# First mixer of a two-block model: projections laid between the delta rule's steps, inverses built from 64x64 blocks, output projection in two halves

## The chip, the core and the metric

The kernel runs on one core of one Trainium2 chip. The metric is the device time of one execution in microseconds (us). TensorE is written PE in the rows (its weight loads PEld), VectorE DVE, ScalarE ACT, GpSimd POOL, and SyncE, which issues most DMAs, SP.

## What is computed

The reference chains two blocks of two layers over 256 tokens (272 with 16 learned ones in front) of width 1024. In the first block a layer is a feed-forward, a mixer and a second feed-forward. The change touches the mixer of layer 0 alone:

```python
def hybrid_attention_mixer(h, w_in, fox_bf, conv_w, a_log, dt_bias, o_gain, w_out):
    fq, fk, fv, ff, gqkv, ga, gb, gz = split_cols(h @ w_in, HYB_SIZES)
    o_fox = forgetting_attention(q_f, k_f, v_f, log_f)[:, :, PAD:]      # 8 heads of 64
    gqkv = jax.nn.silu(causal_depthwise_conv(gqkv, conv_w))
    ...
    o_gdn = gated_delta_rule(q_g, k_g, v_g, log_g, beta)[:, :, PAD:].transpose(0, 2, 1, 3)   # 4 heads of 128
    o_gdn = rms_norm(o_gdn, o_gain) * jax.nn.silu(gz...)
    o = jnp.concatenate([o_fox, o_gdn.reshape(B_, L, GDN_VW)], axis=-1)
    return o @ w_out

def gated_delta_rule(q, k, v, log_g, beta):          # chunks of 128 tokens
    lower = jnp.where(strict, jnp.einsum('bhnid,bhnjd->bhnij', kb, k) * decay, 0.0)
    sol = lax.linalg.triangular_solve(lower, rhs, left_side=True, lower=True, unit_diagonal=True)
    ...
    def step(S, inp):                                # one chunk after the other
        u = u_b - jnp.einsum('bhck,bhkv->bhcv', w_c, S)
        o = jnp.einsum('bhck,bhkv->bhcv', qd, S) + jnp.einsum('bhij,bhjv->bhiv', a_c, u)
        S = S * dl[..., None, None] + jnp.einsum('bhck,bhcv->bhkv', kd, u)
```

## The kernel before, in words

Activations lie feature-major: eight tiles `h[m]` of 128 features by 272 tokens. A matrix product in full precision is three matmuls (`mm3`, lines 105 to 107), since each operand is split into a high and a low part. `wload` (lines 68 to 82) brings a block of weights of 128 x 1024 by DMA into one of four buffers `w`; ACT copies it, 512 columns at a time, to `wh` (line 78), and DVE subtracts that for `wl` (line 79); there are four halves of each. A projection of 128 outputs is thus one DMA, two casts, two subtractions and 24 matmuls of 272 columns into an accumulator of the pool "mm", which has three; all smaller products go to the pool "sm", which has four.

The method `_hybrid` writes the mixer in Python program order, and the tile framework then orders each engine's queue and places the waits; the engines take their queues strictly in order. First come 28 projections: `conv(j)` for twelve blocks of the delta rule's queries, keys and values, `fox(j)` for twelve of the attention's (0 to 3 queries, 4 to 7 keys, 8 to 11 values), and four of `gate`. Short follow-up work is queued by `after(n, f)` and run by the n+1st next `tick`, one tick for each projection: squares and norms (`squared`, `square`, `factors`, `frows`), scaling of queries and keys by four broadcast products for each delta head (`scaled`, line 568), the products inside a chunk (`products`, line 583) and transposes (`turned`). What is still due at the end runs in the loop `while self.due`.

The 272 tokens are the chunks 0, 1 and 2 of 16, 128 and 128. `chunk(i)` inverts a chunk's unit triangular matrices for the four delta heads with `inverse`: from blocks of 1 it doubles up to 128 in seven levels; each level takes a product with `LT` (line 838), a copy of the result to `ivx` on ACT, a second product (line 844), a masked copy on DVE and a transpose (`flip`, lines 827 and 828). `recur` then goes through the chunks: state times keys (672), the inverse applied (678), the state's update (688, 694), the output (698, 699). `finish(i)` norms a chunk's output: squares, sums (714), an inverse root on DVE (lines 160 to 165), diagonals (721), a broadcast product (724), and the scaling and splitting (726 to 729). `attend(j, i)` does one pair of attention heads for one chunk of queries: logits of both heads into two "mm" accumulators (742 to 745), the maximum (746), the exponential (752), transposes (763, 768) and the product with the values (776).

All of these are generators that yield between steps, and the loops at the end of `_hybrid` call them in turn: while there are inverses, the three chunks in each round and one of two attention tasks (pairs 0 and 1, pairs 2 and 3) in every other round; afterwards the recurrence, its norms and the attention. Only then comes the output projection: eight blocks of 24 matmuls (`hyb_w_out`), each added to `h[m]`. `doubled` (line 863) is a second way to invert, for 64x64 blocks, two on the diagonal of a tile, which the RWKV mixer of layer 1 uses; its products (line 873) are pairs of 64x64 matmuls.

## Time and profile before

| | |
|---|---|
| three runs | 3681.22, 3685.11, 3688.15 us; median 3685.11 |
| the profiled execution | 3671.75 us, its span 3669.9 us |
| TensorE matmuls | busy 3590.3 us (98%), 31745 |
| TensorE weight loads | busy 3409.7 us (93%) |
| DVE | busy 2773.0 us (76%) |
| ACT | busy 1942.3 us (53%) |
| POOL | busy 289.1 us (8%) |
| DMA | 561.54 MB, mean 153 GB/s |
| mean granted clock of TensorE | 0.983 of full speed |

The span runs from the first to the last instruction. Matmuls are pipelined and their ends are modelled, so neighbouring ones overlap, and the distance between two starts, not the duration of one, is what a matmul costs in a stream. A busy TensorE can run at either of its two clock levels (2.4 and 1.2 GHz); the granted clock is their mean over a stretch, as a share of the higher.

### The profile page before, as it was taken

The page shows a single profiled execution, that of the slowest core. Times are in us where ns is not written, and L with a number is a line of the kernel's source. Part 1 is how long each engine was busy: PE and PEld are TensorE (multiplying, and loading weights), DVE is VectorE, ACT ScalarE, POOL GpSimd, SP SyncE. Part 2 cuts the span into 40 slices and gives each one's busy share as a digit, 9 for nine tenths or more (in the row PEclk, how much of TensorE's full clock was granted, in tenths as well). Part 3 has the DMA queues.
Part 4 walks back from the last instruction along what each step waited for, and adds up shares of the span by engine and source line. Part 5 has one row for each costly group of instructions (what it writes and reads, how often), then busy time and mean ns, then how long its engine had stood idle before and what let it go on. Part 6 is the DMA issues. An engine that isn't in the chain of part 4 may idle for free. (4 is left out here: it accounts for less than half of the span.)

```text
span 3669.9 us, 80619 instructions
## 1 busy us (share of the span) xinstructions
PE 3590.3 (98%) x31745; PEld 3409.7 (93%) x31745; DVE 2773.0 (76%) x6198; ACT 1942.3 (53%) x4100; POOL 289.1 (8%) x374
## 2 busy tenths in 40 slices
PE   8999999999998999999999999999999999999998
PEld 8999799998898999999999999999989999998887
DVE  6666576667856877788987788657788998788866
ACT  5554355555632557655554444556765555444454
POOL 2111021110201101011000000001011000000000
PEclk9999799999998999999999999999999999999999
DMA  5552055554310565445554444555435555555554
GB/s 184 173 167 81 24 171 172 175 173 127 108 37 25 181 187 172 138 144 168 176 183 164 162 162 161 173 184 164 151 124 182 174 173 173 163 166 173 168 187 150
DMA packets 158426, 561.54 MB, mean 153 GB/s; under 512 B 18715, under 2 KB 21163, under 8 KB 158045
## 3 DMA queue, kind: packets, MB, share of 16 engines
q1 hardware_dynamic: 157628, 555.07, 46.6%
q8 instruction: 248, 4.06, 0.5%
q0 software_dynamic: 416, 1.32, 0.1%
q14 instruction: 134, 1.09, 0.1%
HBM read 555.27 MB, written 1.05 MB: 152 GB/s over the span
## 5 line engine op out<-in xcount | busy, mean ns | idle before, releaser
L78 ACT CAST wh<-w 128x512 fp32r<-128x512 f32 (+1 forms) x2102 | 1292.3, 617 | 1244.3 <-PE mm L106 732.1
L79 DVE TENSOR_TENSOR wl<-w,wh 128x512 fp32r<-128x512 f32 (+1 forms) x2102 | 1461.2, 698 | 559.6 <-ACT wh L78 527.4
L105 PE MATMUL mm<-xh,wh 128*128 128x256 f32 (+2 forms) x4032 | 1162.0, 288 | 12.4 <-ACT wh L78 11.6
L107 PE MATMUL mm<-xh,wl 128*128 128x256 f32 (+2 forms) x4032 | 1152.3, 286 | 21.5 <-DVE wl L79 21.4
L106 PE MATMUL mm<-xl,wh 128*128 128x256 f32 (+2 forms) x4032 | 1141.6, 283 | 0.1
L107 PEld LDWEIGHTS mm<-xh,wl 128*128 128x128 f32 x4032 | 764.2, 190 | 26.9 <-DVE wl L79 25.9
L105 PEld LDWEIGHTS mm<-xh,wh 128*128 128x128 f32 x4032 | 766.5, 190 | 14.9 <-ACT wh L78 12.6
L106 PEld LDWEIGHTS mm<-xl,wh 128*128 128x128 f32 x4032 | 767.8, 190 | 1.8 <-issue 0.6
L2209 PE MATMUL mm<-ah,wh 128*128 128x256 f32 x768 | 219.3, 286 | 0.0
L2209 PE MATMUL mm<-al,wh 128*128 128x256 f32 x768 | 216.9, 283 | 0.0
L2209 PE MATMUL mm<-ah,wl 128*128 128x256 f32 x768 | 215.7, 281 | 0.0
L105 PE MATMUL sm<-xh,wh 128*128 128x272 f32 (+4 forms) x744 | 214.4, 288 | 0.2 <-ACT aa L1072 0.2
L107 PE MATMUL sm<-xh,wl 128*128 128x272 f32 (+4 forms) x744 | 214.1, 288 | 0.0
L106 PE MATMUL sm<-xl,wh 128*128 128x272 f32 (+4 forms) x744 | 213.5, 287 | 0.0
L105 PE MATMUL mm<-ah,wh 128*128 128x272 f32 (+1 forms) x704 | 201.5, 286 | 0.0
L107 PE MATMUL mm<-ah,wl 128*128 128x272 f32 (+1 forms) x704 | 201.4, 286 | 0.0
L106 PE MATMUL mm<-al,wh 128*128 128x272 f32 (+1 forms) x704 | 201.3, 286 | 0.0
L2211 PE MATMUL mm<-wh,ah 128*128 128x512 f32 x384 | 153.5, 400 | 0.0
L2211 PE MATMUL mm<-wh,al 128*128 128x512 f32 x384 | 152.1, 396 | 0.0
L2211 PE MATMUL mm<-wl,ah 128*128 128x512 f32 x384 | 151.1, 394 | 0.0
L2209 PEld LDWEIGHTS mm<-ah,wl 128*128 128x128 f32 x768 | 145.0, 189 | 0.0
L2209 PEld LDWEIGHTS mm<-al,wh 128*128 128x128 f32 x768 | 144.7, 188 | 0.2 <-DVE al L2200 0.2
(866 smaller groups left out, 6774.9 us busy)
## 6 DMA issues: line engine op xcount, KB each, us to landing
w<-p_u SPq DMA_DIRECT2D x256, 512.0 KB, 3.5
w<-p_v SPq DMA_DIRECT2D x256, 512.0 KB, 3.5
w<-ffn_in SPq DMA_DIRECT2D x176, 512.0 KB, 3.5
w<-m_w_in SPq DMA_DIRECT2D x96, 512.0 KB, 3.5
w<-ffn_out SPq DMA_DIRECT2D x64, 448.0 KB, 3.3
w<-ffn_out SPq DMA_DIRECT2D x32, 512.0 KB, 3.5
w<-p_wq SPq DMA_DIRECT2D x32, 512.0 KB, 3.7
w<-hyb_w SPq DMA_DIRECT2D x28, 512.0 KB, 3.5
```

What stands on the lines that cost most here:

```text
L78: self.at_s = nc.scalar.copy(wh, w[:rows, s:e])
L79: self.at_v = nc.vector.tensor_tensor(wl, w[:rows, s:e], wh, op=OP.subtract)
L105: mm(out, wh, xh, start=start, stop=False)
L106: mm(out, wh, xl, start=False, stop=False)
L107: self.at_t = mm(out, wl, xh, start=False, stop=stop)
L2209: M(po[m // 2][:, m % 2 * T : m % 2 * T + T], w_[:, m * P : (m + 1) * P], a_, **flags)
L2211: M(po[m // 2], a_[:, i * P : (i + 1) * P], w_[:, f * 512 : f * 512 + 512], **flags)
```

## The change

Five things are done, all in `_hybrid` and the helpers it calls.

1. Six of the twelve attention projections (the blocks 2, 6, 10, 3, 7 and 11, for pairs 2 and 3) leave the first stretch. `foxes` issues them as generators (`slowly`): the load, twelve matmuls, twelve matmuls, with yields between. The others keep their place; two gates now stand between the last convolutions.
2. The inverses of the chunks 1 and 2 are built from their two 64x64 diagonal blocks by `doubled`, in five levels that keep both the matrix and its transpose (`both=True`), so nothing is flipped; two small products then join the blocks. `Diagonal` picks the blocks out of `LT`. The mask is the 64-wide table.
3. `attend` issues its matmuls by kind: both heads' scores, then both masks, then the rows; with the values, both heads in turn for each block of keys.
4. The attention is a task for each pair; the first two unfinished ones go forward in each round. Pairs 2 and 3 wait until their values are there.
5. The output projection is two halves of twelve matmuls for each block, each with a load of 512 columns and its own addition to `h`: `outs(1)`, the delta rule's half, runs as soon as three chunks are normed, beside the attention that is left; `outs(0)`, the attention's half, at the end.

```diff
+
+
+class Diagonal:
+
+
+    def __init__(self, t):
+        self.t = t
+
+    def __getitem__(self, ix):
+        return self.t[ix[0], ix[1], ix[0]]
...
+            return p[:, :T]
+
+        def slowly(j):
+
+            wh, wl = self.wload(a["hyb_w"][j], KT * P)
+            yield
+            p = self.pmm()
+            for k in range(KT):
+                c = k * P
+                self.mm3(p[:, :T], wh[:, c : c + P], wl[:, c : c + P], xh[k], xl[k], k == 0, k == KT - 1)
+                if k == 3:
+                    yield
             return p[:, :T]
 
...
+        def foxes(js):
+
+            for j in js:
+                p = yield from slowly(16 + j)
+                if j < 8:
+                    V.tensor_tensor((fq, fk)[j // 4][:, j % 4], p, (r8, r)[j // 4], op=OP.mult)
+                else:
+                    o = ht([P, T], "fv", bufs=2)
+                    V.tensor_tensor(o, p, r, op=OP.mult)
+                    yield
+                    fv(j - 8, o)
+                    there.append(j - 8)
+                yield
+
+        there = []
+
         def fv(j, o):
             p = psm()
...
         fox(1)
+        early = [4, 5, 8, 9]
         for j in range(12):
             conv(j)
             if j == 2:
                 decays()
-            if j < 10:
-                fox(j + 2)
-        for j in range(4):
-            gate(j)
+            if j % 2:
+                if early:
+                    fox(early.pop(0))
+                elif j > 8:
+                    gate(j // 2 - 4)
+        gate(2)
+        gate(3)
+        there += [0, 1]
         while self.due:
             tick()
 
+        id64 = ht([P, 64], "id64")
...
         oh, ol = [ht([P, 4, T], "ofh", F32R, tag="rawq")], [ht([P, 4, T], "ofl", F32R, tag="rawk")]
 
...
-            Tt, X = ht([P, 4, n], f"ivt{i}"), ht([P, 4, n], f"ivx{i}")
-            yield from self.inverse(LT[:n], N[:n], Tt[:n], X[:n], mask, n, 4, int(math.log2(n)), psm)
+            if i == 0:
+                Tt, X = ht([P, 4, n], f"ivt{i}"), ht([P, 4, n], f"ivx{i}")
+                yield from self.inverse(LT[:n], N[:n], Tt[:n], X[:n], mask, n, 4, int(math.log2(n)), psm, 64, 6)
+                return
+
+            Nc, Tc, Xc, Lc = (ht([P, 4, 64], f"iv{t}{i}") for t in "abcd")
+            two = slice(0, 64), slice(64, 128)
+            p = psm()
+            for hd in range(4):
+                TR(p[:, hd * P : (hd + 1) * P], LT[:, hd], ident)
+            p = p.rearrange("p (a b) -> p a b", a=4)
+            for t, m, src in ((Nc, 0, LT), (Tc, 6, p)):
+                S.copy(t, id64.unsqueeze(1).to_broadcast([P, 4, 64]))
+                for b in two:
+                    V.copy_predicated(t[b], mask[b, m * 64 : (m + 1) * 64].unsqueeze(1).to_broadcast([64, 4, 64]), src[b, :, b])
+            S.copy(Lc[two[1]], p[two[1], :, two[0]])
+            G.memset(N[two[1], :, two[0]], 0.0)
+            yield
+            yield from self.doubled(Diagonal(LT), Nc, Tc, Xc, mask, 4, 6, psm, both=True)
+            for b in two:
+                G.tensor_copy(N[b, :, b], Nc[b])
+            for A, B, b, dst in ((Lc, Nc, 1, Xc[two[0]]), (Tc, Xc, 0, N[two[0], :, two[1]])):
+                p = psm()
+                for hd in range(4):
+                    M(p[two[0], hd * 64 : (hd + 1) * 64], A[two[b], hd], B[two[b], hd], start=True, stop=True)
+                S.copy(dst, p[two[0], :256].rearrange("p (a b) -> p a b", a=4))
+                yield
...
+            normed.append(i)
...
+            for q, p in enumerate(ps):
+                M(p[:, t0:], idb[:n, :n], fm[:n, :n], start=False, stop=False)
+            for q, p in enumerate(ps):
+                hd = 2 * j + q
                 s = selr[:12, hd * P : hd * P + n]
-                M(p, fq[b, j, t0:nk], fk[b, j, :nk], start=True, stop=False)
-                M(p[:, t0:], idb[:n, :n], fm[:n, :n], start=False, stop=False)
                 M(p, s, rowh[:, :nk], start=False, stop=False)
                 M(p, s, rowl[:, :nk], start=False, stop=True)
...
             p = psm()
-            for q in range(2):
-                b = slice(64 * q, 64 * q + 64)
-                for i2 in range(i + 1):
-                    m = TILES[i2][1]
+            for i2 in range(i + 1):
+                for q in range(2):
+                    b, m = slice(64 * q, 64 * q + 64), TILES[i2][1]
...
 
-        def attention(q):
+        def attention(j):
+            while j not in there:
+                yield
             for i in range(3):
-                for j in (2 * q, 2 * q + 1):
-                    yield from attend(j, i)
-
-        attn = [attention(q) for q in range(2)]
+                yield from attend(j, i)
+            attended.append(j)
+
+        def outs(g):
+
+            while len(attended) < 4 if g == 0 else len(normed) < 3:
+                yield
+            for m in range(KT):
+                wh, wl = self.wload(a["hyb_w_out"][m][:, g * 512 : g * 512 + 512], 512)
+                yield
+                p = self.pmm()
+                for k in range(4):
+                    c = k * P
+                    self.mm3(p[:, :T], wh[:, c : c + P], wl[:, c : c + P], oh[g][:, k], ol[g][:, k], k == 0, k == 3)
+                V.tensor_tensor(h[m], p[:, :T], h[m], op=OP.add)
+                yield
+
+        attended, normed, attn = [], [], []
         inv = [chunk(i) for i in range(3)]
-        n = 0
+        heads = [attention(j) for j in range(4)]
+        dense = [foxes([2, 6, 10, 3, 7, 11])]
         while inv:
             inv = self.round(inv)
-            n += 1
-            attn = (self.round(attn[:1]) if n % 2 else attn[:1]) + (attn[1:] if n % 2 else self.round(attn[1:]))
+            heads[:2] = self.round(heads[:2])
+            dense = self.round(dense)
         oh.append(ht([P, 4, T], "ogh", F32R, tag="kb"))
         ol.append(ht([P, 4, T], "ogl", F32R, tag="qq"))
-        attn.insert(0, recur())
-        while attn:
-            for t in list(attn):
-                if next(t, self) is self:
-                    attn.remove(t)
-
-        for m in range(KT):
-            wh, wl = self.wload(a["hyb_w_out"][m], KT * P)
-            p = self.pmm()
-            for k in range(KT):
-                c = k * P
-                self.mm3(p[:, :T], wh[:, c : c + P], wl[:, c : c + P], oh[k // 4][:, k % 4], ol[k // 4][:, k % 4], k == 0, k == KT - 1)
...
@@ -876,7 +963,7 @@
         for b in range(1, levels):
             S.copy(X, product(LT, Tt))
             yield
-            if b < levels - 1:
+            if both or b < levels - 1:
                 t = product(N, X)
                 n = product(X, N)
```

The new kernel's line numbers are higher: the matmuls of `mm3` are L115 to L117, `product` of `doubled` L960, scores, mask and rows of `attend` L812, L814, L818 and L819, its transposes L837 and L842, values L849, those of `recur` L742 to L769, of `finish` L784 and L794. In the rows `sm` and `mm` are accumulators; `LT`, `nn`, `ivt`, `ivx` matrix, inverse, its transpose and the intermediate product; `ivb` the transposed inverse in 64-wide blocks.

TensorE in one level of the inverses, before:

```order
L844 MATMUL sm_4710<-nn_600_2868,ivx_919_4467 16x16 x4
L844 MATMUL sm_4716<-ivx_921_4471,nn_601_2869 128x128 x4
L844 MATMUL sm_4722<-ivx_923_4475,nn_602_2870 128x128 x4
L827 MATMUL sm_4748<-ident,ivt_920_4470 128x128 x4
L743 LDWEIGHTS idb_2830
L743 MATMUL mm_4864<-fm_2829,idb_2830 128x128
L744 MATMUL mm_4864<-rowh_2847,selr_2831 128x144
L745 MATMUL mm_4864<-rowl_2848,selr_2831 128x144
L827 MATMUL sm_4754<-ident,ivt_922_4474 128x128 x4
```


and in the new kernel:

```order
L116 MATMUL mm_4569<-xl_2783,wh_4475 128x272
L117 MATMUL mm_4569<-xh_2782,wl_4476 128x272
L960 MATMUL sm_4588<-ivb_881_4238,LT_595_2863 64x64 x3
L960 MATMUL sm_4598<-ivb_886_4255,LT_596_2864 64x64 x8
L115 MATMUL mm_4569<-xh_2786,wh_4479 128x272
L116 MATMUL mm_4569<-xl_2787,wh_4479 128x272
```


Between the product with the inverse and the next level stood flips and pieces of logits; now the 64x64 products of both chunks stand inside a projection of 24 matmuls, which is not complete when they are issued.

TensorE early in the recurrence, where the state's first update (`kt`) and the first outputs (`at`) are, before:

```order
L743 MATMUL mm_4993<-fm_2829,idb_2830 128x128
L744 MATMUL mm_4993<-rowh_2847,selr_2831 128x144
L688 MATMUL sm_4950<-u_1025_4936,kt_605_2873 128x128 x4
L699 MATMUL sm_4957<-at_597_2865,u_4934 128x16 x4
L776 MATMUL sm_4963<-pt_4938,vt_612_2880 64x128
L776 MATMUL sm_4963<-pt_4938,vt_613_2881 64x128
```


and in the new kernel:

```order
L758 MATMUL sm_5094<-u_1034_5076,kt_605_2873 128x128 x4
L769 MATMUL sm_5101<-at_597_2865,u_5074 128x16 x4
L115 MATMUL mm_5081<-xh_2786,wh_5063 128x272
L116 MATMUL mm_5081<-xl_2787,wh_5063 128x272
L117 MATMUL mm_5081<-xh_2786,wl_5064 128x272
L115 MATMUL mm_5081<-xh_2790,wh_5063 128x272
L116 MATMUL mm_5081<-xl_2791,wh_5063 128x272
L784 MATMUL sm_5109<-ones,ivx_1039_5107 16x1 x4
L842 MATMUL sm_5131<-ident,L_5040 16x16 x2
```


Behind these two products stood the attention's products with values; now dense matmuls of a projection stand there, and between them the sums of the first chunk's norm (`ones,ivx`).

TensorE at the second chunk's norm, before:

```order
L744 MATMUL mm_5228<-rowh_2847,selr_2831 128x272
L745 MATMUL mm_5228<-rowl_2848,selr_2831 128x272
L742 MATMUL mm_5317<-fk_2879,fq_2878 128x272
L724 MATMUL sm_5201<-ivt_1085_5196,ones 128x128 x4
L698 MATMUL sm_5210<-qd_2860,st_5088 128x128
L699 MATMUL sm_5210<-at_599_2867,u_5167 128x128
```


and in the new kernel:

```order
L784 MATMUL sm_5250<-ones,ivx_1069_5248 128x1 x4
L742 MATMUL sm_5287<-st_5233,kn_2861 128x128 x4
L812 MATMUL mm_5397<-fk_2879,fq_2878 128x272
L814 LDWEIGHTS idb_2830
L814 MATMUL mm_5397<-fm_2829,idb_2830 128x128
L818 MATMUL mm_5397<-rowh_2847,selr_2831 128x272
L819 MATMUL mm_5397<-rowl_2848,selr_2831 128x272
L794 MATMUL sm_5301<-ivt_1076_5296,ones 128x128 x4
L837 MATMUL sm_5311<-ident,L_5198 128x128 x2
L842 MATMUL sm_5315<-ident,L_5198 16x128 x2
```


Between the sums of the norm (L714) and its broadcast product (`ivt` with `ones`, L724) stood some twenty rows: the inverse applied to the last chunk, logits of several heads and a pair's values, of which the last rows are shown. Now only the state's product with the keys and one head's logits stand there, and no dense matmul follows until the output half.

## Rows read from the trace of the kernel before

**Rows 1.** Timeline of TensorE: start, duration, instruction; first and last of the first mixer.

```profile
214.68 0.29 PE L105 MATMUL mm<-xh,wh 128*128 128x272 f32 x1
214.81 0.29 PE L106 MATMUL mm<-xl,wh 128*128 128x272 f32 x1
...
466.07 0.29 PE L105 MATMUL mm<-xh,wh 128*128 128x272 f32 x1
```

**Rows 2.** Stretch, length; busy PE, PEld, DVE, ACT, POOL (count); clock, DMA share, GB/s.

```profile
215.00:321.10 106.10, 104.72 (x818) 99.42 (x816) 85.23 (x204) 59.73 (x141) 30.51 (x48) 1.00 0.48 156
...
333.00:373.00 40.00, 39.83 (x370) 34.58 (x369) 17.14 (x60) 18.52 (x54) 0.00 (x0) 1.00 0.00 1
373.00:430.00 57.00, 55.34 (x269) 40.01 (x268) 25.48 (x109) 13.40 (x42) 0.00 (x0) 0.72 0.00 1
430.00:442.50 12.50, 11.64 (x64) 8.35 (x64) 6.30 (x23) 3.27 (x9) 0.00 (x0) 0.78 0.00 1
```

**Rows 3.** Timeline of TensorE in the inverses, one level of both big chunks.

```profile
355.49 1.95 PE L838 MATMUL sm<-ivt,LT 128*128 128x128 f32 x16
357.28 2.05 PE L844 MATMUL sm<-ivx,nn 128*128 128x128 f32 x16
...
359.39 0.66 PE L827 MATMUL sm<-ident,ivt 128*128 128x128 f32 x4
```

**Rows 4.** Timeline of TensorE in the RWKV mixer: 64x64 products, and changes of shape.

```profile
1048.41 1.10 PE L873 MATMUL sm<-N,X 64*64 64x64 f32 x32
1049.34 1.10 PE L873 MATMUL sm<-X,N 64*64 64x64 f32 x32
...
1055.86 0.28 PE L107 MATMUL mm<-gh,wl 128*128 128x256 f32 x1
1056.07 0.38 PE L105 MATMUL mm<-gh,wh 32*128 32x256 f32 x1
```

**Rows 5.** Timeline of TensorE in the attention: two heads’ logits, one pair’s values.

```profile
420.55 0.72 PE L742 MATMUL mm<-fk,fq 64*128 64x272 f32 x2
421.80 0.72 PE L742 MATMUL mm<-fk,fq 64*128 64x272 f32 x2
...
437.78 1.95 PE L776 MATMUL sm<-pt,vt 16*64 16x128 f32 x12
```

**Rows 6.** Waits of TensorE from 373 to 444, weight loads, then matmuls: total, times, longest.

```profile
PEld sm L776 <- issue: 5.3, 25, 0.3
...
PE mm L742 <- ACT L L752: 0.6, 1, 0.6
```

**Rows 7.** Timeline of TensorE in the RWKV mixer: 64-row products, row groups in turn.

```profile
1006.96 2.05 PE L1223 MATMUL sm<-AR,BK 64*128 64x128 f32 x30
```

**Rows 8.** DMA issues by line: size of one, median us to landing.

```profile
w<-hyb_w SPq DMA_DIRECT2D x28, 512.0 KB, 3.5
```

**Rows 9.** Groups of DVE in the projections: count, busy us, mean ns, idle before.

```profile
L79 DVE TENSOR_TENSOR wl<-w,wh 128x512 fp32r<-128x512 f32 x63 | 47.7, 760 | 18.6 <-ACT wh L78 17.9
L517 DVE SCALAR_TENSOR_TENSOR cy<-xpad,col,cy 128x272 f32<-128x272 f32 x36 | 17.9, 498 | 1.0 <-ACT cy L515 0.2
L513 DVE TENSOR_TENSOR xpad<-mm,rs 128x272 f32<-128x272 f32 x12 | 5.2, 432 | 0.2 <-PE mm L107 0.2
```

**Rows 10.** The same groups of DVE in the recurrence: the norm of a chunk.

```profile
L721 DVE TENSOR_SCALAR ivt<-ident,rs 128x128 f32<-128x128 f32 x8 | 1.7, 277 | 0.0
L726 DVE TENSOR_TENSOR og<-og,sm 128x512 f32<-128x512 f32 x2 | 1.4, 688 | 4.3 <-PE sm L724 4.3
...
L165 DVE SCALAR_TENSOR_TENSOR rs<-rqt,rs 128x4 f32<-128x4 f32 x6 | 0.9, 157 | 0.1
```

**Rows 11.** Timeline of TensorE in the recurrence: a wait before a pair’s logits.

```profile
388.87 0.51 PE L742 MATMUL mm<-fk,fq 64*128 64x144 f32 x2 [0.62 <-ACT L L752]
```

**Rows 12.** Groups from 333 to 444.4 that free an accumulator of logits.

```profile
L752 ACT ACTIVATE L<-mm,mc 128x272 f32<-128x272 f32 x8 | 3.9, 489 | 3.7 <-DVE mc L750 3.7
...
L746 DVE TENSOR_REDUCE mx<-mm 128x1 f32<-128x272 f32 x8 | 3.5, 441 | 5.1 <-PE mm L745 4.8
```

More of the change, by code (lines that the diff above doesn't have):

```diff
@@ L382, in _hybrid @@
         xh, xl, r = self.prep(h, g, T)
-        mask = self.konst(hp, "mask", U8, 12)
+        mask = self.konst(hp, "mask64", U8, 12)
         tri = self.konst(hp, "tri")
@@ L739, in attend @@
             for q, p in enumerate(ps):
-                hd, b = 2 * j + q, slice(64 * q, 64 * q + 64)
+                b = slice(64 * q, 64 * q + 64)
+                M(p, fq[b, j, t0:nk], fk[b, j, :nk], start=True, stop=False)
+            for q, p in enumerate(ps):
+                M(p[:, t0:], idb[:n, :n], fm[:n, :n], start=False, stop=False)
+            for q, p in enumerate(ps):
+                hd = 2 * j + q
                 s = selr[:12, hd * P : hd * P + n]
-                M(p, fq[b, j, t0:nk], fk[b, j, :nk], start=True, stop=False)
-                M(p[:, t0:], idb[:n, :n], fm[:n, :n], start=False, stop=False)
                 M(p, s, rowh[:, :nk], start=False, stop=False)
@@ L794, in _hybrid @@
         ol.append(ht([P, 4, T], "ogl", F32R, tag="qq"))
[L795 to L807 removed]
+        chain = [recur()]
@@ L809, in cols_in @@
+        dense.append(outs(1))
+        while chain or attn or heads:
+            chain = self.round(chain)
+            attn[:] = self.round(attn)
+            heads[:2] = self.round(heads[:2])
+            dense[:1] = self.round(dense[:1])
+        for t in dense + [outs(0)]:
+            for _ in t:
+                pass
     def cols_in(self, pool, src, n):
@@ L812, in cols_in, with inverse @@
         return t
-    def inverse(self, LT, N, Tt, X, mask, n, H, levels, psm):
+    def inverse(self, LT, N, Tt, X, mask, n, H, levels, psm, W=P, nl=7):
         nc = self.nc
@@ L821, in inverse @@
         v3 = lambda p: p[:n, : H * n].rearrange("p (a b) -> p a b", a=H)
-        mk = lambda b, t=0: mask[:n, (7 * t + b) * P : (7 * t + b) * P + n].unsqueeze(1).to_broadcast([n, H, n])
+        mk = lambda b, t=0: mask[:n, (nl * t + b) * W : (nl * t + b) * W + n].unsqueeze(1).to_broadcast([n, H, n])
         def flip(dst, src):
@@ L860, in base, with doubled @@
             V.copy_predicated(t, mask[:, m * 64 : (m + 1) * 64].unsqueeze(1).to_broadcast([P, H, 64]), src)
-    def doubled(self, LT, N, Tt, X, mask, H, levels, psm):
+    def doubled(self, LT, N, Tt, X, mask, H, levels, psm, both=False):
         V, S, M = self.nc.vector, self.nc.scalar, self.nc.tensor.matmul
```

2 lines of the change are left out of this document (1 added, 1 removed).

## Prediction

> **What bounds the kernel now.** I read the times by stretch first. The first mixer fills 214.7 to 466.1 of the span [rows 1], from its first projection matmul to the first matmul of the next feed-forward: 251.4 us. Outside it both kernels issue the same instructions in the same order, but for a few small copies drawn into the feed-forward ahead of it, so the whole difference has to arise here. By stretch [rows 2]: the projections (215 to 321.1) run at a full clock with the matmul engine nearly always busy; so do the products behind them and the inverses (333 to 373). The recurrence (373 to 430) and the start of the output projection (430 to 442.5) do not: the mean granted clock is 0.72 and 0.78, with 269 and 64 matmuls in 57.0 and 12.5 us, and DVE busy for 25.5 and 6.3. "Busy" misleads there: at a half clock the same matmul counts twice. The loss is 57.0 x 0.28 + 12.5 x 0.22 = 18.7 us by clock, and 1.7 + 0.9 = 2.6 us idle: **21.3 us** that other matmul work could have used. The reader should see that TensorE, by work or by its clock, sets every stretch, and that only one has room.
>
> **What the change does to the sum.** Negative is faster.
>
> *The inverses.* One level now costs 1.8 us (355.49 to 357.28), 2.0 and two flips of 0.6 each, for both big chunks [rows 3]: 5.0. Five levels, a last one without flips (3.8) and the first flips (1.2) make 30. Afterwards a product of four heads in 64x64 blocks is half of the RWKV mixer's product of eight heads, whose starts are 0.93 apart [rows 4]: 0.47. Five levels x three products x two chunks = 14.1; two transposes of 0.6 and four small joining products, which I put at 0.4, make 2.8. So 17 in place of 30: I take -12.5 for what can't be timed exactly. Against it stands the change of array shape: dense 128x128 matmuls now stand between 64x64 ones. In [rows 4] a shape change (128 rows, then 32) puts 0.21 between starts, instead of 0.125 within one shape [rows 1]: about 0.1. I count 16 runs of 64x64 products in the new order, 32 changes: +3.2. Sum **-9.3** (bounds -12.5 with changes free, -6 with them doubled).
>
> The Trainium skill, "TensorEngine Tiling (Array Packing)", Key Properties, says that a change of the tiling mode, as against a change of tile, drains the engine. If each of the 32 changes drained a whole matmul (0.29 long, started 0.125 after the one before), the term would be 5.3 instead of 3.2, and the gain 2 us smaller; the trace shows the 0.1, and its rows agree with the rule in kind only.
>
> *The order inside a pair of heads.* Logits of the two heads now stand next to each other, and so do the two heads' products with the values. Before, a head's logits take 1.25 us (420.55 to 421.80), the values of a last block 1.9 [rows 5], and the weight loads of the latter waited 5.3 us for "issue" in all [rows 6]. Alternating 64-row products [rows 7] start 2.05/30 = 0.065 us apart instead of the 1.79/16 = 0.11 of [rows 3], so pairs may overlap. For four pairs at most 1.4 (logits) + 3.2 (fewer shape changes) + 5 (values) = 9.6; nothing at least, since the order breaks some of the pairs up. I take **-6**, nearer the upper end because fewer changes are certain.
>
> *Six projections move.* Each is 24 matmuls 0.125 us apart [rows 1]: 3.0 us, 18.1 in all. They leave 215 to 321 and return as twelve halves among the inverses and the recurrence; half of the output projection (8 x 12 matmuls, 12 us) comes before the attention is through. Their work on TensorE is unchanged. Each brings its load (512 KB, 3.5 us to land [rows 8]; the output halves are 16 of 256 KB instead of 8 of 512), two casts and two subtractions. No transfer runs in 333 to 430 [rows 2], and four weight buffers hold at least 6 us of matmuls, so loads cost nothing; if that cover went, a landing of 3.5 us would stand in front of a piece. ACT and DVE have half of 373 to 430 free. The smaller mask, the block copies on POOL and the added 64-wide identity are waited for by nobody soon. What this move can give back is the lost time: **-21.3**.
>
> *What will still be lost.* **+22**, from the new order of each queue:
> - Projections, 3 (0 to 7). The last eight are four convolutions and four gates. DVE: 16 subtractions x 0.76, 4 x (0.43 + 3 x 0.50), 4 x about 1.1 and about 5 for the norm factors [rows 9] = 29 us, against 24 of matmuls. Buffers of two projections absorb part.
> - Behind them, 3 (1 to 6). All four scaling steps, not two, now follow the last gate; 16 products of 0.43 on DVE are 6.9 us against 4.1 of matmuls.
> - Inverses, 4 (2 to 10). Eight masked copies and the tables of both chunks on DVE precede the first product; later rounds are covered by the twelve-matmul pieces.
> - Recurrence, 11 (8 to 22). Early steps have a dense piece behind each wait. From the second chunk's norm on none is left: the pieces have run out and the output half waits for the last norm. There the inverse root is eleven operations of about 0.16, then come four diagonals of 0.28 and three of 0.7 [rows 10]. I count waits of 0.5, 1.6, 3, 0.4, 1.6, 3.5 and 1 along the new order = 11.6. The upper end adds that some 11 us of matmuls there run at a half clock.
> - End, 1 (0 to 2). In the last eight halves DVE has 0.43 + 0.76 + 0.50 = 1.7 us a block [rows 9] against 1.5.
>
> Sum: -9.3 - 6 - 21.3 + 22 = **-14.6 us**. The profiled execution took 3671.75 us, 1.85 more than its span; it becomes 3657.2. The three runs have a median of 3685.11, 13.4 above it; taking the difference over to them, **3670.5**. A measurement of this kernel can tell about 0.2%, 7.4 us, from no change.
>
> **Rivals.**
> - *The matmul engine stays packed.* If the waits stand at their lower ends (11 us in all) and the order inside pairs gives all 9.6, the sum is -9.3 - 9.6 - 21.3 + 11 = -29: 3656. For: TensorE is never short of work before 373 [rows 2]. Against: the chain of the last two norms has nothing beside it.
> - *The clock stays down.* If waits of 3 us hold the recurrence at its present clock, it loses 21 instead of 11, and the inverses 6 instead of 4: -2.6, no change to a measurement, 3682.5. For: in the old kernel such waits (0.62 before 388.87 [rows 11]) stand in the stretch with the clock of 0.72. Against: thirty microseconds of dense work now lie in between.
> - *Slower: three accumulator tiles.* The "mm" pool has three. A dense piece holds one over a yield, a pair's logits take two, and two pairs now run in step, so five are wanted. TensorE is in order; a piece behind a taken tile holds everything, the recurrence too. A tile comes free after two maxima of 0.44, an exponential of 0.49 [rows 12] and two operations of 0.16 [rows 10]: 1.7 us. Twenty pieces stand between logits. With all waits uncovered it costs 34; from 13 on the gain turns into a loss of over 7.4 (22 us); at 15, 25.5 us, 3696. For: the old kernel knows the wait. Against: it shows 0.6 us of it [rows 6], and the new order puts transposes or products between.
> - That the change doesn't move what it says is ruled out by the order shown.
>
> **How the numbers follow.** Forecast, 7.5 to 25 us faster: 0.56. Packed engine: 0.14. Clock stays down: 0.20. Accumulators: 0.10. So faster 0.70, no change 0.20, slower 0.10. The bounds give -32 to +16. Leaving out the third case and half of the first, the range is 3655 to 3685; the likeliest case alone covers 3660 to 3677.
>
> **What would show it.** Right: the mixer's stretch is some 237 us; the last gate ends near 303; the first 64x64 product near 317; the recurrence begins about 372, as before, but both first pairs of heads are then done; the granted clock in the recurrence is above 0.85, with dips only at the two last norms. Each product of four heads takes about 0.47. The output projection ends near 451. Wrong: TensorE waits on ACT's exponentials in front of dense pieces (accumulators); a recurrence clock near 0.72 (clock); waits on DVE's subtraction before 303 of over 7 us (the projections are DVE's); or a shape change that costs far more than 0.1.

## The result and the profile after

The changed kernel took 3652.87 us in the median of five runs (3648.88 to 3664.90), the kernel before 3685.18 (five runs). The medians are 32.3 us apart; the ratio on record, 0.992 with a 95% interval of 0.9899 to 0.9940, stands for some 29 us. Four more runs, beside later experiments, had a median of 3654.26 against 3683.17 (0.9919; 0.9904 to 0.9934). The profiled execution took 3648.88 us, its span 3647.1. So the kernel is faster, as forecast, but by about twice the forecast 14.6 us: the median lies 2.1 us under the prediction's range of 3655 to 3685, the mean of the five runs (3656.03) just inside it.

The mixer was forecast to take 237 us. The timeline of TensorE gives its first matmul and the first of the next feed-forward, as [rows 1] did:

```profile
214.28 0.29 PE L115 MATMUL mm<-xh,wh 128*128 128x272 f32 x1
...
451.66 0.29 PE L115 MATMUL mm<-xh,wh 128*128 128x272 f32 x1
```

That is 237.4 us instead of 251.4: 14.0 less. The sum was right for the mixer; part of what it was made of, and what came on top of it outside the mixer, was not. The stretches, with the columns of [rows 2]:

```profile
215.00:302.70 87.70, 83.17 (x649) 78.23 (x647) 73.86 (x178) 50.21 (x123) 30.16 (x50) 1.00 0.45 148
302.70:321.10 18.40, 18.40 (x139) 16.63 (x137) 15.06 (x38) 3.00 (x9) 0.00 (x0) 0.72 0.13 46
321.10:372.50 51.40, 51.40 (x786) 43.38 (x784) 27.58 (x88) 18.95 (x62) 1.63 (x4) 0.93 0.06 18
372.50:390.00 17.50, 17.50 (x148) 15.94 (x144) 12.98 (x54) 5.93 (x19) 0.00 (x0) 1.00 0.20 63
390.00:430.00 40.00, 34.33 (x194) 26.58 (x192) 19.98 (x77) 11.06 (x32) 0.00 (x0) 0.70 0.08 26
430.00:451.66 21.66, 21.66 (x175) 20.96 (x175) 17.92 (x39) 14.22 (x31) 4.25 (x5) 1.00 0.51 161
...
373.00:430.00 57.00, 51.33 (x334) 42.12 (x331) 32.46 (x128) 16.83 (x50) 0.00 (x0) 0.79 0.12 38
```

The last gate ends at 302.7 (303 was said), the recurrence begins at 372.5 (372), the output projection ends at 451.7 (451). Two other signs missed: the first 64x64 product starts at 321.2, not near 317, and the clock of the old recurrence's stretch (373 to 430, last row) is 0.79, not above 0.85. And the lost time is all there again: the clock is 0.72 between the last gate and the inverses, and from 390 on, when the six projections have run out, it is 0.70 with 5.7 us idle. Up to 390 the recurrence runs at a full clock, where the old one had 0.72 [rows 2].

The waits of TensorE from 214 to 452 (total, times, longest):

```profile
PE sm L794 <- DVE ivt L791: 4.2, 2, 2.8
PE sm L578 <- DVE fac L572: 2.8, 1, 2.8
PE sm L784 <- ACT ivx L781: 1.3, 1, 1.3
```

L791 and L781 belong to a chunk's norm, L572 to the norm factors of queries and keys. No accumulator of logits is waited for any more (0.6 us before [rows 6]).

Rows of TensorE's timeline show the new parts: two products of four heads in 64x64 blocks (one chunk) 0.46 us apart where the old ones of both chunks stood 1.8 and 2.0 apart [rows 3]; the first logits products of both heads in 0.73 us, where those of one head took 0.72; and the values of two pairs in 1.97 us, where one pair took 1.95 [rows 5].

```profile
352.62 0.63 PE L960 MATMUL sm<-iva,ivc 64*64 64x64 f32 x16
353.08 0.63 PE L960 MATMUL sm<-ivc,iva 64*64 64x64 f32 x16
...
354.11 0.73 PE L812 MATMUL mm<-fk,fq 64*128 64x272 f32 x4
354.77 0.29 PE L814 MATMUL mm<-fm,idb 128*128 128x128 bf16 x2
...
365.68 1.97 PE L849 MATMUL sm<-pt,vt 16*64 16x128 f32 x24
```

### The profile page after: what moved, and what is told of

Same layout as the page of the kernel before. It is cut to its first block, busy times and chain, and to the rows that moved or that the text cites. A ratio compares the mean times of both kernels' runs of the same rounds, so it can differ in the third digit from the quotient of the medians.

```text
span 3647.1 us, 81225 instructions
## 1 busy us (share of the span) xinstructions
PE 3558.8 (98%) x32025; PEld 3384.5 (93%) x32025; DVE 2782.1 (76%) x6221; ACT 1934.2 (53%) x4093; POOL 296.8 (8%) x380
## 3 DMA queue, kind: packets, MB, share of 16 engines
HBM read 554.75 MB, written 1.05 MB: 152 GB/s over the span
## 5 line engine op out<-in xcount | busy, mean ns | idle before, releaser
L117 PE MATMUL mm<-xh,wl 128*128 128x256 f32 (+2 forms) x4032 | 1151.2, 286 | 23.0 <-DVE wl L89 22.9
L115 PE MATMUL mm<-xh,wh 128*128 128x256 f32 (+2 forms) x4032 | 1161.1, 288 | 12.9 <-ACT wh L88 12.3
L117 PEld LDWEIGHTS mm<-xh,wl 128*128 128x128 f32 x4032 | 762.6, 189 | 28.8 <-DVE wl L89 28.2
L115 PEld LDWEIGHTS mm<-xh,wh 128*128 128x128 f32 x4032 | 764.9, 190 | 16.3 <-ACT wh L88 13.1
L2296 PE MATMUL mm<-al,wh 128*128 128x256 f32 x768 | 216.9, 283 | 0.0
L115 PE MATMUL sm<-xh,wh 128*128 128x272 f32 (+4 forms) x744 | 214.5, 288 | 0.0
L117 PE MATMUL sm<-xh,wl 128*128 128x272 f32 (+4 forms) x744 | 214.1, 288 | 0.0
L116 PE MATMUL sm<-xl,wh 128*128 128x272 f32 (+4 forms) x744 | 213.4, 287 | 0.0
L115 PE MATMUL mm<-ah,wh 128*128 128x272 f32 (+1 forms) x704 | 201.5, 286 | 0.0
L117 PE MATMUL mm<-ah,wl 128*128 128x272 f32 (+1 forms) x704 | 201.4, 286 | 0.0
```

The source lines that it names most:

```text
L115: mm(out, wh, xh, start=start, stop=False)
L116: mm(out, wh, xl, start=False, stop=False)
L117: self.at_t = mm(out, wl, xh, start=False, stop=stop)
L2296: M(po[m // 2][:, m % 2 * T : m % 2 * T + T], w_[:, m * P : (m + 1) * P], a_, **flags)
```

## Experiments

**How they are compared.** A run's time mixes the mixer with clock losses elsewhere (below), so each kernel's profile is read in three numbers: the mixer's length; what it loses by clock (23 or so stretches of about 10 us, each its length times one less its granted clock, added up); and the difference, its length at a full clock, which still holds the time that TensorE waits. Both kernels were profiled twice:

| kernel | mixer, us | lost by clock | at full clock | runs' median (range) |
|---|---|---|---|---|
| before | 251.4 | 20.5 | 230.9 | 3685.18 (3681.22 to 3688.77) |
| before, again | 255.8 | 25.7 | 230.1 | 3669.96, the profiled execution |
| order inside a pair alone | 244.6 | 22.2 | 222.4 | 3657.35 (3653.97 to 3664.05) |
| 64x64 blocks alone | 246.4 | 25.6 | 220.8 | 3671.06 (3662.44 to 3678.01) |
| both, nothing moved | 239.5 | 25.5 | 214.0 | 3660.09 (3651.60 to 3667.82) |
| changed | 237.4 | 20.5 | 216.9 | 3652.87 (3648.88 to 3664.90) |
| changed, again | 238.4 | 20.3 | 218.1 | 3654.26 (3650.25 to 3661.02) |
| changed, old order in a pair | 249.0 | 22.2 | 226.8 | 3674.52 (3663.53 to 3679.16) |
| changed, old inverses | 254.0 | 27.2 | 226.8 | 3670.03 (3666.98 to 3680.48) |
| changed, output undivided | 233.7 | 18.9 | 214.8 | 3646.80 (3644.43 to 3649.81) |
| changed, early quarter | 230.7 | 11.9 | 218.8 | 3656.82 (3652.12 to 3664.73) |
| the same, pieces from the scaling on | 247.3 | 27.4 | 219.9 | 3673.92 (3669.69 to 3680.33) |
| early quarter, a half last | 230.4 | 17.0 | 213.4 | 3655.78 (3653.40 to 3662.16) |
| the same, one projection back | 232.6 | 15.4 | 217.2 | 3656.31 (3648.16 to 3662.56) |

Length at a full clock repeats within 0.8 and 1.2 us where the mixer itself moves by 4.4 and 1.0. Every other kernel was profiled once, so a difference of 4 us between two mixers is not beyond doubt. Times of the kernel before beside the experiments had medians of 3679.93 to 3683.17.

**One part alone.** `attend` of the change put into the kernel before (the matmuls abbreviated):

```diff
-            for q, p in enumerate(ps):
-                M(p, fq..., fk...); M(p[:, t0:], idb, fm); M(p, s, rowh); M(p, s, rowl)
+            for q, p in enumerate(ps): M(p, fq..., fk...)
+            for q, p in enumerate(ps): M(p[:, t0:], idb, fm)
+            for q, p in enumerate(ps): M(p, s, rowh); M(p, s, rowl)
...
-            for q in range(2):
-                for i2 in range(i + 1):
+            for i2 in range(i + 1):
+                for q in range(2):
```

> The kernel before with one part of the change: logits and value products of a pair of heads in the new order. The first mixer takes 251.4 us in the trace of before and 237.4 in that of the change (214.28 to 451.66). Theory A (the prediction's sum): this part is worth 6 us of matmul work, so the mixer falls to about 245. Theory B (from the trace of the changed kernel: a pair's last logits there take 1.57 us from start to start instead of 2.5, a pair's last values 0.95 instead of 1.9): it is worth about 9, the mixer falls to 242. Rival: much of the attention stands in the recurrence, where TensorE has room, and what it saves there is swallowed: 249 or more.

Mixer 244.6, 6.8 less than in the first profile before; at a full clock 8.1 less than the mean of the two profiles before (230.5). Theory A by the mixer, theory B by the full clock; nothing is swallowed.

The new `chunk`, `inverse`, `doubled` and the smaller mask put into the kernel before (cut to the two calls):

```diff
...
-            yield from self.inverse(LT[:n], N[:n], Tt[:n], X[:n], mask, n, 4, int(math.log2(n)), psm)
...
+            yield from self.doubled(Diagonal(LT), Nc, Tc, Xc, mask, 4, 6, psm, both=True)
...
```

> The kernel before with one part of the change: the inverses of the two big chunks from 64x64 blocks. Theory A: matmul work falls by 12.5 us and nothing comes against it, as no dense piece stands between the products here (the shape changes of the sum belong to those): mixer 239. Theory B: there are fewer rounds, so less of the attention is done beside the inverses and more of it in the recurrence; the gain is still that of the work, 9 to 12, as TensorE sets both stretches: 239 to 242. Rival: with fewer rounds the waits for the masked copies come bare and eat half: 246 or more, with idle time of TensorE of over 3 us between 321 and the recurrence, where the trace of before has 0.2.

At a full clock 9.7 less, but 25.6 lost by clock. Against the first profile before (20.5 lost) only 5.0 of it shows, 246.4; against the second, which lost as much by clock (25.7), 9.4. So how much of the saving the mixer keeps is not settled. The time is the rival's, but not by its waits: from 321 to 373 TensorE idles 1.2 us. Its mean clock there is 0.83 (0.97 before): the inverses are over at 361, and the recurrence behind them runs at 0.54 up to 373.

Both together, and nothing moved:

> The kernel before with the 64x64 inverses and the new order inside a pair, and no projection or output half moved. Alone the two gave 5.0 and 6.8 us in the mixer. Theory A: they add up, mixer 239 to 240, so that moving projections and halves is worth 2 to 3 us of the change's 14. Theory B: the prediction's balance of what the move fills and what it still loses (+0.7) holds, and the mixer takes about 237. Rival: the two need the moved projections, since without them the saved matmul work only turns into waits and a lower clock: 243 or more, with more than 27 us lost by clock in the mixer (20.5 in the kernel before).

239.5, theory A: 16.5 less at a full clock, nearly the 17.8 of the two added. The runs don't add up so: their medians are 25.4 us (order), 11.7 (blocks) and 19.8 (both) under those of the kernel before beside them, and 25.4 is far more than the order takes off the mixer; the whole runs' mean clock differs too (0.987, 0.981 and 0.983 in the median). The windows show where the time now goes, and why there is something to fill:

```profile
321.00:357.00 36.00, 34.76 (x725) 31.38 (x725) 25.49 (x86) 11.40 (x44) 1.57 (x4) 1.00 0.08 30
357.00:420.00 63.00, 59.26 (x279) 45.12 (x278) 28.05 (x127) 13.16 (x47) 0.00 (x0) 0.61 0.00 1
```

The inverses are over at 357, and the recurrence takes 63 us at a clock of 0.61: with less work on TensorE its clock falls further than the old 0.72 [rows 2].

**One part undone.** The same two edits, reversed in the changed kernel:

> The changed kernel with the old order of the logits and value products. Theory A: the mixer grows from 237.4 by 6 us to 243.4. Theory B: by 9, to 246.4. Rival: the extra matmul work falls into the 5.7 us that TensorE idles between 390 and 430 and lifts its clock there, so that the mixer grows by less than 4, to 241 at most.

> The changed kernel with the old 128x128 inverses, all else as changed. Theory A: the 32 changes of array shape cost 3.2, so that undoing gives back 9.3 us: 246.7. Theory B: the changes cost next to nothing, and undoing costs 12 or more: 249.5. Rival: the longer inverses take more rounds, so that pieces of the projections and of the attention move out of the recurrence into them; the recurrence then has less beside it and its clock falls under the 0.79 that the changed kernel has between 373 and 430: 252 or more.

Each costs 9.3 us at a full clock (226.8 against the mean of 217.5). Without the new order the mixer grows by 11.1 us over the mean of the two profiles of the change (237.9), without the blocks by 16.1. In the latter the rival is right: it loses 27.2 by clock and takes 254.0, longer than in the first profile before, though TensorE has the new order's savings, and 9.4 longer than the same kernel with nothing moved (244.6). Its recurrence (stretch, length, busy PE, PEld, DVE, ACT, POOL, clock, DMA share, GB/s):

```profile
386.60:440.00 53.40, 46.01 (x241) 35.57 (x241) 24.48 (x109) 12.22 (x38) 0.00 (x0) 0.65 0.02 7
```

The old inverses take more rounds; the projections are used up in them, and the recurrence is left with a clock of 0.65 and 7.4 us idle. With the short inverses the move takes the mixer from 239.5 to 237.9: 5.1 less lost by clock, 3.4 more idle (10.2 instead of 6.8). Those 1.6 us are fewer than the 4.4 between two profiles of one kernel, so a gain of the whole move is not shown; a part of it gains more (output projection undivided, below).

**The unchanged kernels once more.**

> The kernel before, unchanged, for a second profiled execution. The first took 3671.75 us, less than any of its runs without a profile (3675.84 to 3688.15). Theory A: the mixer is as long as before (251.4, within 1), and what differs is the clock that TensorE is granted in stretches that no kernel here changes, the end of the RWKV mixer above all (15.3 us lost by clock there in the first profile, 3.5 in that of the changed kernel): executions of the same kernel differ by 5 to 15 us there. Rival: the mixer itself takes a longer form in most executions, 258 to 265, and the gain of the change in the mixer is larger than the two profiles show.

> The changed kernel again, for a second profiled execution and more runs. Theory A: the mixer less what it loses by clock repeats within 1 us (216.9 in the first profile; the kernel before gave 230.9 and 230.1), the mixer itself within 5 (237.4), and the end of the RWKV mixer loses either 3.5 or about 15 us by clock, so that executions fall between 3647 and 3665. Rival: the first profile was a lucky draw in the mixer too, and it takes 243 or more.

The mixer of the kernel before took 255.8, 3.4 more than theory A allowed, all of it by clock (25.7 against 20.5); the changed kernel repeated it within 1.0. At the end of the RWKV mixer (60 us, from 674 us behind the end of the first mixer; busy PE, clock, DMA) the changed kernel showed both outcomes. First profile, then second:

```profile
1125.66:1185.66 60.00, 53.10 (x489) 0.94 0.23 73
```

```profile
1127.89:1187.89 60.00, 55.28 (x435) 0.74 0.17 54
```

The kernel before gave 0.74 both times. No instruction there differs between the two kernels. In time it is some 7 us: the same matmul (L115, `mm<-X1o,wh`) starts 720.1 us behind the mixer's end in the first profile of the change, 727.1 in its second, and 726.7 in the first of the kernel before. This is how the two outcomes part, the timeline of the kernel before and of the changed one (first profile):

```profile
1154.75 0.68 PE L1348 MATMUL sm<-UV,G 128*64 128x64 f32 x8 [0.46 <-ACT Y L1354]
1155.36 0.84 PE L1352 MATMUL sm<-st,AR 64*64 64x64 f32 x8
1156.13 0.58 PE L105 MATMUL mm<-Tt0o,wh 128*128 128x256 f32 x1
```

```profile
1140.64 0.68 PE L1435 MATMUL sm<-UV,G 128*64 128x64 f32 x8 [0.46 <-ACT Y L1441]
1141.25 0.68 PE L1439 MATMUL sm<-st,AR 64*64 64x64 f32 x8
1141.85 0.38 PE L115 MATMUL mm<-Tt0o,wh 128*128 128x256 f32 x1
```

The same instructions, the same 0.61 us between the first two, the same wait of 0.46 us: in the one TensorE falls to its lower level inside the second row, in the other it does not; what came ahead of these rows and made the difference is not shown.

**Output projection undivided.** The changed kernel with the old loop of eight blocks of 24 matmuls at the end:

```diff
-        dense.append(outs(1))
...
-        for t in dense + [outs(0)]:
+        for t in dense:
             for _ in t:
                 pass
+        for m in range(KT):
+            wh, wl = self.wload(a["hyb_w_out"][m], KT * P)
...
```

> The changed kernel with the output projection undivided at the end, as in the kernel before. Theory A (the prediction: the halves fill time that is lost): in the changed kernel five of the delta rule's pieces stand beside the attention of the last two pairs, 414 to 435; without them that stretch waits or falls to a half clock: mixer 241 to 246. Theory B: the attention there needs no cover, the same matmuls only come later: 236 to 239. Rival: half as many additions and loads make the end shorter: under 236.

The rival's time came: 233.7, 4 us less than with halves, and 3646.8 us in the median, a ratio of 0.9902 (0.9887 to 0.9917). It has the lowest median here, and three of its four runs lie under all nine of the changed kernel; the intervals overlap. Against the kernel with both parts and nothing moved (239.5; ratio 0.9936 to 0.9969) the moved projections are worth 5.8 us of mixer, by clock (18.9 lost instead of 25.5), and the runs agree. The halves then give 4 of it back, 3.6 as idle time (10.2 instead of 6.6). The timeline shows where. The changed kernel, from the last products of the recurrence to the first half piece:

```profile
404.10 0.39 PE L769 MATMUL sm<-at,u 128*128 128x128 f32 x2
405.82 1.05 PE L784 MATMUL sm<-ones,ivx 128*128 128x1 f32 x8 [1.34 <-ACT ivx L781]
409.71 2.04 PE L794 MATMUL sm<-ivt,ones 128*128 128x128 f32 x8 [2.84 <-DVE ivt L791]
...
414.50 0.60 PE L115 MATMUL mm<-ogh,wh 128*128 128x272 f32 x1
...
416.08 0.85 PE L812 MATMUL mm<-fk,fq 64*128 64x144 f32 x2
```

The kernel with the undivided output:

```profile
410.24 0.39 PE L769 MATMUL sm<-at,u 128*128 128x128 f32 x2
410.55 0.51 PE L812 MATMUL mm<-fk,fq 64*128 64x144 f32 x2
...
412.25 1.00 PE L784 MATMUL sm<-ones,ivx 128*128 128x1 f32 x8
...
414.67 0.28 PE L819 MATMUL mm<-rowl,selr 12*128 12x272 f32 x1
414.88 0.39 PE L115 MATMUL mm<-ofh,wh 128*128 128x272 f32 x1
...
416.78 2.02 PE L794 MATMUL sm<-ivt,ones 128*128 128x128 f32 x8 [0.42 <-DVE ivt L791]
```

The logits (L812 to L819) that stand beside the last norm here stand behind the first matmul of the first half piece there, and that piece needs the norm's result. TensorE takes its queue in order; so the piece that was to fill a hole keeps out the logits that would have filled it. They are not alone: the first matmuls of the undivided output (`ofh`, from 414.88), which need the attention only, stand ahead of the last norm's product too, while the change keeps the attention's half for the end. TensorE's wait for the norms (L794) is 1.4 us here and 4.2 there. Which of the two fillers counts, and what the rival named, the 16 loads and 16 additions instead of 8, costs by itself, was not tried.

**More pieces.** The attention's half split again, the first two pairs' quarter right behind the last projection:

```diff
-        dense.append(outs(1))
+        dense += [outs(0, range(2)), outs(1)]
...
-        for t in dense + [outs(0)]:
+        for t in dense + [outs(0, range(2, 4))]:
```

> The changed kernel with one more split: the attention's half of the output projection in two quarters, and that of the first two pairs goes into the list of dense pieces right behind the last projection, ahead of the half of the delta rule (eight pieces of six matmuls of 0.125 us). Theory A (the recurrence loses time because its dense pieces run out): these 6 us of matmuls fill the hole between 395 and 415, where the changed kernel idles 5.5 us and has a clock of 0.7: the mixer takes 228 to 232 instead of 237.4. Theory B (the chain of the two last norms sets the end there, over ScalarE and VectorE): casts and subtractions of the new pieces stand in its way and the pieces only shift; 235 to 239. Rival: eight more additions and smaller loads cost more than is filled: over 239.

Theory A: the mixer is 230.7 and the recurrence's stretch is nearly full, a clock of 0.94 from 373 to 430 where the change has 0.79 over the same stretch:

```profile
373.00:430.00 57.00, 55.88 (x421) 48.03 (x420) 39.02 (x155) 21.92 (x65) 0.00 (x0) 0.94 0.17 54
430.00:445.17 15.17, 11.15 (x89) 10.93 (x88) 12.74 (x28) 9.60 (x25) 4.87 (x15) 1.00 0.58 190
```

At the end of the mixer TensorE waits 4.0 us in one piece for a cast of the next feed-forward's weights, behind the split of its input on ACT and DVE. A half at the end instead of eight quarters takes that wait away:

```diff
-        for t in dense + [outs(0, range(2, 4))]:
-            for _ in t:
-                pass
+        dense.append(outs(0, range(2, 4)))
+        while dense:
+            dense = self.round(dense)
+            dense[1:] = self.round(dense[1:])
```

> The kernel with the early quarter, and behind the attention the quarter pieces of the last two pairs alternate with what is left of the delta rule's half, two quarters to one half, so that a half comes last. In the kernel with the early quarter (mixer 230.7) the last eight pieces are quarters of 0.75 us each, while ScalarE and VectorE need over 1 us a block to split the next feed-forward's input, and TensorE waits 4.0 us at the end of the mixer. Theory A: those 4.0 us go: mixer 226 to 228. Theory B: the input's split is bound by ScalarE and VectorE over the whole tail, and the wait only moves: 230 to 232. In both the run's time follows the mixer only within the 10 us by which executions differ behind it: 3640 to 3660.

The idle time between 430 and the end falls from 4.0 to 0.2 us and the length at a full clock to 213.4, the lowest here; but this profile lost 17.0 by clock instead of 11.9, and the mixer stays at 230.4. The runs of neither kernel follow: 3656.82 and 3655.78, no less than the change. Between the mixer's end and the end of the span their profiles have 3208.2 and 3208.6 us, 12.8 and 13.2 more than the first profile of the change (3195.4) but about 3 more than its second (3205.4), so most of that is within what one kernel shows. Starting the pieces earlier, or giving one projection back, did not help:

```diff
+        dense = [foxes([2, 6, 10, 3, 7, 11])]
         while self.due:
             tick()
+            dense = self.round(dense)
...
-        dense = [foxes([2, 6, 10, 3, 7, 11])]
         while inv:
```

> As the one before, and in addition the dense pieces begin with the scaling steps, ahead of the inverses, where the changed kernel has a clock of 0.72 between 302.7 and 321.1. Theory A (any dense matmuls there lift the clock): 5 us lost there fall to under 2, and the mixer takes 2 to 4 less than without it. Theory B (matmul time is conserved: pieces taken from the inverses and the recurrence leave the same hole there): no change within 1.5. Rival: the casts and subtractions of the pieces delay VectorE's 16 products there, which the inverses wait for: 2 or more longer.

```diff
+        fox(2)
         gate(2)
...
-        dense = [foxes([2, 6, 10, 3, 7, 11])]
+        dense = [foxes([6, 10, 3, 7, 11])]
```

> As the one before, with one of the six moved projections put back ahead of the last two gates. Theory A (the wait of 2.8 us for the norm factors at 299.4, and the half clock from 305.8 that follows it, come from VectorE being short of time in the last eight projections): one more light projection there covers the wait and keeps the clock: 3 to 7 us less than without it. Theory B (TensorE's work is conserved, and the recurrence has enough pieces): within 2 us of it. Rival: VectorE only gets two more subtractions there (0.7 each), and the pieces miss in the recurrence: 2 or more longer.

The first took 247.3, the rival: the first 64x64 product comes at 334.6 instead of 321.4. The second took 232.6, 2.2 us more than the kernel without it, by a hair the rival's; one profile of each can't tell that from theory B. Its first product came at 325.1 instead of 322.0, 3 us later, as the projection put back takes.

## Why the prediction was right, and where not

**Direction and sum.** The mixer's 14.0 us (by the second profiles 17.4) answer to the 14.6 of the sum. Its terms:

- *Inverses, -9.3.* Measured at a full clock: -9.7 put into the kernel before, -9.3 taken out of the changed one. So the total was right. Its two halves these runs don't part: in TensorE's order the 64x64 products stand in 16 groups with 32 changes of shape in the change, as counted, 10 of them next to a projection's dense matmuls; but in the kernel with the blocks alone there are still 12 groups and 24 changes, so that kernel does not measure the products without changes. Rows of the change price one beside dense matmuls:

```profile
321.20 0.32 PE L960 MATMUL sm<-ivb,LT 64*64 64x64 f32 x2
...
321.69 0.29 PE L115 MATMUL mm<-xh,wh 128*128 128x272 f32 x1
321.90 0.68 PE L960 MATMUL sm<-ivb,LT 64*64 64x64 f32 x14
322.51 0.39 PE L116 MATMUL mm<-xl,wh 128*128 128x272 f32 x1
322.74 0.29 PE L117 MATMUL mm<-xh,wl 128*128 128x272 f32 x1
```

From 321.69 to 322.74 are 1.05 us. Two dense matmuls at 0.125 and fourteen small ones (sixteen take 0.46) make 0.65, so the two changes cost 0.40: 0.2 each, where the sum took 0.1 and the full drain (5.3 for 32) 0.17. What the other 22 cost, and what the products alone saved, stays open.
- *Order inside a pair, -6.* Undersized: -8.1 and -9.3, next to the upper end of 9.6. Two heads' logits side by side take the time of one, which the prediction's overlap of pairs allowed for and did not take in full.
- *What moved work fills, -21.3, and what is still lost, +22.* The balance held nearly (+0.7 said; the mixer went from 239.5 to the mean of 237.9), but not for the reason given. The old hole was filled up to 390, and a new one nearly as large came behind it. Item by item: projections 4.5 idle (3 said; 87.70 less 83.17), behind them 18.40 x 0.28 = 5.2 (3), inverses 51.40 x 0.07 = 3.6 (4), recurrence 40.00 x 0.30 = 12.0 by clock and 5.7 idle = 17.7 (11), end 0 (1): 31 instead of 22. The term most mis-sized is the recurrence's, 17.7 for 11: the waits were counted there at full-clock prices, and 12.0 of the 17.7 are clock, which only the upper end of 22 had in it. With dense pieces beside these waits (early quarter) the clock of the stretch was 0.94.

So the mixer's sum owes its closeness in part to luck: the errors cancel. Each mixer less its clock loss and its idle time (4.1 and 10.2 us) makes 226.8 and 206.7: TensorE's work fell by 20.1, not 15.3, and what is lost rose by 6.1, not 0.7. Idle time at a half clock counts twice in that, so it is rough.

**The size of the whole.** "So the whole difference has to arise here" is the step that failed. In the first profiles 14.0 us arise in the mixer, 0.4 ahead of it and 8.4 behind it, where nothing was changed: the end of the RWKV mixer (664 to 734 us behind the end of the first) lost 15.3 us by clock in one and 3.5 in the other, some 7 us of time (above). The profiled execution before was moreover a good one, 13.4 us under its runs' median, and that of the change only 4.0 under its own; the prediction carried the 13.4 over to both. The mean granted clock of whole executions says the same: 0.978 to 0.984, median 0.981, in 44 runs of the kernel before, and 0.981 to 0.987, median 0.986, in the nine of the change. What that is worth the runs show themselves: a straight line through the 44 has 2.4 us for each 0.001 of clock, one through the nine 2.3. By this estimate the 0.005 are some 12 us of the 29 to 32 gained, and at an equal clock of 0.983 the lines lie 15.8 us apart (3675.7 and 3660.0), about what the mixer's profiles differ by. Where the runs without a trace lose the clock could not be seen.

**Rivals.** The packed engine did not come (10.2 us idle in the mixer), though its time, 3656, is the nearest to the measured one. The clock that stays down came for the second half of the recurrence and was paid for by the larger savings. The accumulators were not waited for; but their idea, a dense piece that holds up the logits behind it in TensorE's queue, is what the divided output does.

**Left open.** Why the same instructions get one clock or the other behind the mixer, and whether a kernel can choose: the change, the old inverses, both parts with nothing moved and the undivided output had the good outcome (3.4 or 3.5 us lost), the rest 13.7 to 17.1, the change itself both. No order of the mixer's end times separates them: 453.9 had the bad outcome and 454.2 the good one.

## What to carry to other kernels

Judge an edit by the stage's length less what its clock takes, and profile each kernel twice: here that number repeated within about 1 us, while unchanged code behind the mixer took 3195.4 us in one profile of a kernel and 3205.4 in the other. Moved matmul work is worth something only as long as it lasts to the end of the hole: count how many pieces are left at each wait, and look in the queue for what a piece that waits keeps behind it. And shorten the work first: the two plain savings gave nearly all of the mixer's gain (239.5 of 251.4 to 237.4), and without the shorter inverses the move made it longer.

## What was not expected of the hardware

**VectorE held by GpSimd.** In the changed kernel's projections, VectorE's small operations on 24 or 12 columns take 0.15 to 0.18 us, but four on the way to the norm factors took 0.75 to 0.79. Each ended when a GpSimd operation did (timeline of DVE, then of POOL):

```profile
292.48 0.79 DVE L175 SCALAR_TENSOR_TENSOR rt<-rqs,rt 128x24 f32<-128x24 f32 x1
293.61 0.75 DVE L173 SCALAR_TENSOR_TENSOR rqs<-nt,rt 128x24 f32<-128x24 f32 x1
...
297.04 0.76 DVE L175 SCALAR_TENSOR_TENSOR rt<-rqs,rt 128x24 f32<-128x24 f32 x1
...
297.88 0.76 DVE L569 TENSOR_SCALAR fac<-rt 128x12 f32<-128x12 f32 x1
```

```profile
292.04 1.20 POOL L543 TENSOR_TENSOR cth<-cth,cy 128x272 f32<-128x272 f32 x1 [4.72 <-ACT cth L541]
293.31 1.01 POOL L544 TENSOR_TENSOR rawv<-cth,cy 128x272 f32<-128x272 f32 x1
296.95 0.81 POOL L543 TENSOR_TENSOR cth<-cth,cy 128x272 f32<-128x272 f32 x1 [2.63 <-ACT cth L541]
297.84 0.78 POOL L544 TENSOR_TENSOR rawv<-cth,cy 128x272 f32<-128x272 f32 x1
```

293.27 against 293.24, 294.36 against 294.32, 297.80 against 297.76, 298.64 against 298.62. The four cost some 0.6 each, 2.4 us together, and TensorE's longest wait in the projections, 2.8 us, is for the factors they lead to. That taking them apart would end the wait was not tried. The Trainium skill, "SBUF — State Buffer", "Who interferes with whom", says that VectorE and GpSimd share a pair of ports that one holds for its whole instruction while the other waits, and that a VectorE instruction needs the pair when it has two inputs in SBUF or runs in a two-port mode. Three of the four rows, with two inputs each, agree; the fourth (L569) has one, and no row shows its mode.

**A clock drawn by the execution.** The end of the RWKV mixer at 0.94 or 0.74, with the same instructions and the same waits ahead of it. The Trainium skill, "TensorE: Matmul & The Clock Gate", "Part 1: The HAM clock gate", says that the chip looks at TensorE's activity in a window that runs freely and does not start with the kernel, so that one kernel can get different clocks; the two profiles of the change agree with that in kind, and no run here shows the window itself.
